# Seven products of quarters in the output half of the last feed-forward layer

## The chip, the cores and the metric

The kernel runs on one core of a Trainium2 chip. The core has a matrix engine (TensorE, PE in the profile, with its weight loads as PEld), three engines for elementwise work (VectorE, DVE; ScalarE, ACT; GpSimd, POOL), SyncE (SP), whose queue issues the transfers, and sixteen transfer engines. Each engine takes its instructions in order and waits for the others through semaphores. On-chip data lie in SBUF; matmuls add into PSUM, eight banks of 512 fp32 columns on 128 partitions. The metric is the time of one execution on the device, in microseconds (us).

## The reference

Two layers over 512 latent tokens of width 1024. The change is in the feed-forward part of the second layer, on latent tokens alone:

```python
def swiglu(h, w_in, w_out):
    gate, up = jnp.split(h @ w_in, 2, axis=-1)
    return (jax.nn.silu(gate) * up) @ w_out
...
f_l = swiglu(modulate(rmsnorm(x, norm_g[i, 2]), sh_fl, sc_fl), ffn_w_in[i], ffn_w_out[i])
x = x + g_fl * rmsnorm(f_l, norm_g[i, 3])
```

The hidden width is 2816. The output half is `act @ w_out`, a product of 512 x 2816 by 2816 x 1024, all in fp32. It is the last matmul of the kernel: after it come one norm, a gain, the addition to x, and the store.

## The kernel before

Every fp32 matrix is split into a high part, which the matmul takes whole, and a low part, the rest. `high` (line 216) is a cast on ScalarE, `low` (line 219) a subtraction on VectorE; a product takes three matmuls: high by high, high by low, low by high (`mm_a`, line 268). Weights come in units of 256 rows by 1024 columns (1 MB) from the list `w`; unit 77 is the first of the eleven of this layer's `w_out` (`F2`, line 36). `Stream` (`ws`, from line 276) fetches units into two buffers `raw` and splits them in halves of 128 rows, each into one of four buffers `w_hi` and `w_lo`. `staged` (line 1092) splits the activations of one 128-row chunk for all 512 tokens into one of four stage buffers `stg` (high part 512 columns, low part 512). Other shared buffers: two `big` ones, six of 1024 columns called `vec`.

`down` (line 1166) is the output half. A unit is two chunks of 128 rows; for each of four blocks of 128 tokens (t) and both halves of 512 output columns, unit and block take 2 x 3 x 2 = 12 matmuls of 128 stationary by 512 moving columns. The eight results y (t, half) fill all eight PSUM banks. Units 0 to 8 run one after the other over the four blocks; the last two units run block by block, so that each block's norm and store (`Chain`, steps `square_y`, `rstd_y`, `gain_y`, `add_x`, `store`) can follow while the next block is multiplied.

`FFN.rest` (line 1501) is the input half. It computes chunk n of the hidden activations (n = 2 to 21), each by seven products of quarters of the input matrix (`product`, line 1433); `gates` (line 1468) writes the chunk, and `act` (line 1290) gives its place: pairs of chunks in one buffer of 2 x 512 columns. T = 10.08 is the planned time of a chunk. The last product of chunk 21 runs after the first output block (`lead`, line 1538), so that the output half begins at the planned time b = T x 20 there.

The order of the work is written by hand: `at(time, step, ...)` (line 582) notes a step with a planned time, or with a rank in a list of names, and `run_plan` (line 592) emits all noted steps in that order. Inside `tc.manual_schedule()` each engine's instructions keep the order in which they are emitted. From the input half of the last layer to the first output block, and again for the last two units, this holds; between these, the units of `down` are ordered by the compiler's own scheduler. The planned times only order the steps: an instruction runs as soon as its engine is free and what it needs is there.

Of the kernel before, what the change touches and what calls it, by code (L numbers as in the profile page):

```python
# [203 lines left out]
def backbone_kernel(ctx: ExitStack, tc: tile.TileContext, a, out):  # L204
# [11 lines left out]
    def high(hi, src):  # L216
        nc.scalar.copy(out=hi, in_=src)  # L217
# [1063 lines left out]
    class FFN:  # L1281
        def __init__(self, layer):
            self.layer, self.u0, self.head_ps, self.slot, self.bank = layer, F1[layer], {}, slot, slot

        def open(self, H):
            self.cm = pool(f"ffn{self.layer}")
            self.p = self.cm.__enter__()
            self.H, self.pairs = H, {}

        def act(self, n):  # L1290

            if n // 2 not in self.pairs:
                self.pairs[n // 2] = self.p.tile([P, 2 * SEQ], F32, name="act", tag="act", bufs=NFF // 2)
            return self.pairs[n // 2][:, (n % 2) * SEQ:(n % 2 + 1) * SEQ]

        def lend(self, u):

            for i in range(2):
                ws.lend(u + i, [self.p.tile([P, D], F32R, name="w_lent", tag="act", bufs=NFF // 2) for _ in range(4)])

        def head(self, t, n):

# [163 lines left out]
            nc.scalar.activation(out=self.g[n][:, i * 256:(i + 1) * 256], in_=self.ps[n, 0 if i else 2], func=AF.Silu)  # L1466

        def gates(self, n):
            nc.vector.tensor_tensor(out=self.act(n), in0=self.c.pop(n)[:, 512:], in1=self.g.pop(n), op=ALU.mult)

        def prepare(self, ch):

# [28 lines left out]
        def rest(self, nxt_of, head, **kw):  # L1501

            T, last, u0, f2 = 10.08, NFF - 1, self.u0, F2[self.layer]
            at(.1, self.head_turn, *self.prev)
            for n in range(2, NFF):
                b = T * (n - 2)
                order = (1, 5, 4, 6, 2, 3, 7) if n > 2 else (1, 2, 5, 6, 3, 7)
                for i, p in enumerate(order):
                    at(b + T / 7 * i, self.product, n - 1 if p == 4 else n, p)
                at(b + 1.7, self.keep, n, 0)  # L1510
                at(b + (3.15 if n > 2 else 4.5), self.keep, n, 1)
                at(b + 6, self.keep, n, 2)
# [12 lines left out]
                at(b + 9.1, ws.fetch, u0 + n + 2 if n < last - 1 else f2 + n - last + 1)  # L1525
            m5 = Ada(self.layer, 5)
            at(T + 5.3, m5.start, nc.gpsimd)
            for k in range(KC):
                at(T * (1 + 2 * k) + 5, m5.fetch_chunk, k)
                at(T * (4 + 2 * k) + .5, m5.add_chunk, k)  # L1530
            at(T * 17, m5.fetch_gain)
            for z in range(2):
                b = T * (18 + z)
                at(b + 2, m5.halve, z * 512, nc.vector)
                at(b + 5.7, m5.total, z * 512, self.bank)
                at(b + 6.6, m5.done, z * 512)

            def lead(take, work):
# [11 lines left out]
            down(f2, NFF // 2, lambda k: staged(self.act(k)), lambda: V[self.layer, 5], nxt_of, head, lead=lead, **kw)  # L1550


    f0 = FFN(0)
# [305 lines left out]
```

## Time and profile before

| | |
|---|---|
| three runs, us | 1137.48, 1137.61, 1141.35 (median 1137.61) |
| profiled execution, us | 1139.76 |
| its span, first to last instruction | 1138.0 |
| granted TensorE clock, mean | 0.999 |
| PE, DVE, ACT, POOL busy, share of the span | 98%, 78%, 50%, 44% |
| first output block of the last layer starts | 1010.7 us |

All rows of the profile come from the one profiled execution. An instruction's duration runs from its start until its result is written; instructions of one engine overlap a little, so back to back they cost less than their durations. Names like `y<-w_hi,st` tell what an instruction writes and reads; L272 is a line of the kernel, and for helpers such as `high` (L217), `low` (L220) and `mm_a` (L272) it is the helper's. "Idle before" is the time in which the engine waited just before an instruction, with the instruction or transfer that ended the wait.

### The profile page before, as it was taken

What the parts mean: (1) busy time and instruction counts of PE and PEld (TensorE: products, weight loads), DVE (VectorE), ACT (ScalarE), POOL (GpSimd) and SP (SyncE); (2) the same over time, 40 slices, a digit from 0 to 9 for tenths busy, and PEclk for the clock granted to TensorE, in tenths of its full rate; (3) what the DMA queues carried; (4) which work ended last, traced back from release to release, by engine and by line L of the source; (5) the groups of instructions that cost most, each with busy time, mean ns of one, the idle gap of its engine ahead of it and who ended that gap; (6) DMA issues with size and microseconds to landing.
All of it is one profiled execution on the core that took longest, in us unless ns stands there. A gap on an engine that the chain in (4) does not pass through costs nothing.

```text
span 1138.0 us, 17909 instructions
## 1 busy us (share of the span) xinstructions
PE 1117.8 (98%) x7134; PEld 984.5 (87%) x7134; DVE 887.5 (78%) x1140; ACT 565.5 (50%) x983; POOL 499.6 (44%) x341
## 2 busy tenths in 40 slices
PE   8999999999999999999999999999999999999997
PEld 5788877768899999998888888888899999998886
DVE  6888988959988989988855767847999998953325
ACT  6357778666544455543324544435545555533322
POOL 2347565514677767630001314006588888700000
PEclk9999999999999999999999999999999999999999
DMA  9642332233134233368753265331243333323221
GB/s 371 261 154 83 123 108 78 75 141 110 65 131 148 97 131 144 130 221 314 297 185 111 77 220 183 119 114 47 70 159 127 113 145 130 131 88 135 74 74 74
DMA packets 29528, 158.19 MB, mean 139 GB/s; under 512 B 3450, under 2 KB 7802, under 8 KB 13700
## 3 DMA queue, kind: packets, MB, share of 16 engines
q1 hardware_dynamic: 29444, 157.04, 38.2%
q8 instruction: 56, 0.92, 0.3%
q14 instruction: 28, 0.23, 0.1%
HBM read 154.94 MB, written 2.10 MB: 138 GB/s over the span
## 4 chain that ended last, share of the span: by engine, by line
PE 88%; DVE 7%; issue 2%; ACT 2%; DMA 1%; SPq 0%; POOL 0%; DVEq 0%; POOLq 0%; ACTq 0%
PE f L1442 33%; PE y L272 27%; PE v L272 3%; PE s_ps L888 3%; PE o_ps L941 2%; PE pT_ps L921 2%; PE u L1684 1%; PE u L1686 1%; PE u L1685 1%; PE q_ps L264 1%; PE q_ps L266 1%; PE q_ps L265 1%; DVE w_lo L220 1%; PE kv L264 1%; DVE a_sum L1368 1%
## 5 line engine op out<-in xcount | busy, mean ns | idle before, releaser
L272 PE MATMUL y<-w_hi,st 128*128 128x512 f32 x928 | 251.4, 389 | 0.0
L220 DVE TENSOR_TENSOR w_lo<-w_raw,w_hi 128x1024 fp32r<-128x1024 f32 (+1 forms) x109 | 154.6, 1419 | 103.6 <-ACT w_hi L217 103.6
L217 ACT CAST w_hi<-w_raw 128x1024 fp32r<-128x1024 f32 x122 | 127.7, 1052 | 177.7 <-PE y L272 124.5
L272 PEld LDWEIGHTS y<-w_hi,st 128*128 128x128 f32 x928 | 173.9, 188 | 36.0
L1399 POOL TENSOR_TENSOR T<-w_raw 128x512 f32<-128x512 f32 x80 | 144.9, 1831 | 96.0 <-DMA w_raw<-in_w 60.5
L1442 PE MATMUL f<-H,w_hi 128*128 128x256 f32 x960 | 178.3, 283 | 2.8 <-DVE fc L1453 2.8
L220 DVE TENSOR_TENSOR w_lo<-T,w_hi 128x1024 fp32r<-128x1024 f32 x80 | 149.0, 1862 | 5.6 <-ACT w_hi L217 5.5
L1442 PEld LDWEIGHTS f<-H,w_hi 128*128 128x128 f32 x960 | 150.1, 192 | 3.7 <-DVE fc L1453 3.2
L245 POOL TENSOR_TENSOR ry<-ry,mhalf 128x1 f32<-128x1 f32 x16 | 9.2, 576 | 327.2 <-DVE ry L242 188.8
L272 PE MATMUL y<-w_lo,st 128*128 128x512 f32 x464 | 144.2, 389 | 0.0
L1442 PE MATMUL f<-H,w_lo 128*128 128x256 f32 x480 | 135.8, 283 | 0.0
L1442 PE MATMUL f<-S,w_hi 128*128 128x256 f32 x640 | 120.0, 285 | 0.3 <-ACT fc L1449 0.3
L217 ACT CAST w_hi<-T 128x1024 fp32r<-128x1024 f32 x80 | 83.6, 1046 | 55.1 <-PE f L1442 29.7
L1449 ACT COPY fc<-f 128x256 f32<-128x256 f32 x120 | 44.8, 373 | 122.9 <-PE f L1442 120.5
L272 PEld LDWEIGHTS y<-w_lo,st 128*128 128x128 f32 x464 | 87.0, 188 | 18.0
L1442 PEld LDWEIGHTS f<-S,w_hi 128*128 128x128 f32 x640 | 99.5, 191 | 0.9 <-ACT fc L1449 0.5
L1442 PEld LDWEIGHTS f<-H,w_lo 128*128 128x128 f32 x480 | 92.1, 192 | 0.0
L1442 PE MATMUL f<-S,w_lo 128*128 128x256 f32 x320 | 90.7, 284 | 0.5 <-DVE w_lo L220 0.5
L366 DVE SCALAR_TENSOR_TENSOR acc<-ada_raw,sc,acc 128x1024 f32<-128x1024 f32 x64 | 84.8, 1325 | 6.4 <-DMA ada_raw<-in_ada 4.2
L1399 POOL TENSOR_TENSOR T<-w_raw,T 128x512 f32<-128x512 f32 x40 | 82.6, 2066 | 3.1
L1399 POOL TENSOR_TENSOR T<-T,w_raw 128x512 f32<-128x512 f32 x40 | 76.3, 1908 | 3.1
L915 POOL TENSOR_SCALAR p<-p,st 128x512 f32<-128x512 f32 (+1 forms) x64 | 55.7, 884 | 42.8 <-DVE st L911 25.1
(238 smaller groups left out, 2437.2 us busy)
## 6 DMA issues: line engine op xcount, KB each, us to landing
w_raw<-in_w SPq DMA_DIRECT2D x83, 1024.0 KB, 4.9
ada_raw<-in_ada SPq DMA_DIRECT2D x32, 1024.0 KB, 4.9
ada<-in_ada SPq DMA_DIRECT2D x8, 1024.0 KB, 12.0
ada_k<-in_ada SPq DMA_DIRECT2D x16, 512.0 KB, 5.7
w_raw<-in_w SPq DMA_DIRECT2D x10, 512.0 KB, 3.7
row<-in_norm_g SPq DMA_DIRECT2D x7, 512.0 KB, 6.5
xin<-in_x SPq DMA_DIRECT2D x4, 512.0 KB
x<-in_x SPq DMA_DIRECT2D x4, 512.0 KB, 7.2
```

What stands on the lines that cost most here:

```text
L217: nc.scalar.copy(out=hi, in_=src)
L220: (eng or nc.vector).tensor_tensor(out=lo, in0=src, in1=hi.bitcast(F32), op=ALU.subtract)
L264: nc.tensor.matmul(dst, lh, rh, start=first, stop=False)
L272: nc.tensor.matmul(dst, l, w[:, n * 512:(n + 1) * 512], start=first and i == 0, stop=last and i == 2)
L366: nc.vector.scalar_tensor_tensor(out=ac, in0=w, scalar=sc[:, k:k + 1], in1=ac, op0=ALU.mult, op1=ALU.add)
L888: nc.tensor.matmul(dst, self.qT[:, j, :], keys, start=i == 0, stop=i == 1)
L915: nc.gpsimd.tensor_scalar(out=p, in0=p, scalar1=self.st[:, 12 + j:13 + j], scalar2=1.0, op0=ALU.mult, op1=ALU.mult)
L921: nc.tensor.transpose(ps[:, j * P:(j + 1) * P], self.probs[j][:, i * P:(i + 1) * P], ident)
L941: nc.tensor.matmul(self.o[z * HD:(z + 1) * HD, c], v, pt[:, c], start=i < 2, stop=i >= self.nb - 2, tile_position=(0, z * HD), skip_group_ ...
L1399: nc.gpsimd.tensor_tensor(out=T[i], in0=x, in1=y, op=op)
L1442: nc.tensor.matmul(dst, l[:, w], r[:, k, :], start=first and k == 0 and j == 0, stop=k == 3 and j == 2, skip_group_check=True)
L1449: nc.scalar.copy(out=self.c[n][:, i * 256:(i + 1) * 256], in_=self.ps[n, 1 if i == 1 else 0])
```

## The change

In the last layer only, units 1 to 8 of the output half (2048 of the 2816 rows) are multiplied by seven products of quarters instead of eight. Units 0, 9 and 10 stay as they were.

- The activations A of units 1 to 8 are kept in four buffers of four quarters of 512 columns: even or odd chunk by the first or second 256 tokens (`fours`, `act`). Buffer p holds two units. The weights B are cut the same way: even or odd chunk by the first or second 512 output columns, and fetched so, 4 units x 512 columns (1 MB) at a time (`fetch7`, eight transfers).
- The seven products, in the order 1, 2, 7, 6, 3, 5, 4, each go over p = 0 to 3; one p is a block of twelve matmuls (`product7`). Per block, `a7_high` and `w7_high` cast a token quarter (512 columns) and a weight quarter (1024 columns) on ScalarE, `a7_low` and `w7_low` subtract on VectorE. They are planned 4.5, 3.9, 3.8 and 2.9 us ahead of the block (U = 2.72).
- Products 7, 6, 3 and 5 take sums of token quarters, made in place by `s7` on VectorE, planned 4.6 us ahead of the block. Products 7 and 5 take sums of two weight quarters, made by `t7` on VectorE; for products 6 and 4, another quarter is added to the sum of product 7 by an accumulating transfer that GpSimd issues (`t7_add`, eight of 512 KB).
- Products 1, 7, 6 and 5 add up in the same two banks. Between them ScalarE saves the state (`save7`), and VectorE adds the saved parts to the banks of the other quarters (`add7`). Unit 0 is multiplied first, in the order of blocks 2, 3, 0, 1, as starting value.
- Units 9 and 10 follow block by block with the norms as before (`plain7`). All of it is noted with `at` and emitted in that order, inside the manual schedule.

```diff
+        def fours(self, g, of=F32):
+            return self.p.tile([P, 2 * D], of, name="act4" if of is F32 else "w_lent", tag="act4", bufs=4)
...
+            if self.fast and 1 <= u < 9:
+                g = (u - 1) // 2
+                if g not in self.four:
+                    self.four[g] = self.fours(g)
+                return self.four[g].rearrange("p (q u s) -> p q u s", q=4, u=2)[:, 2 * (n % 2):2 * (n % 2) + 2, (u - 1) % 2, :]
...
         def gates(self, n):
-            nc.vector.tensor_tensor(out=self.act(n), in0=self.c.pop(n)[:, 512:], in1=self.g.pop(n), op=ALU.mult)
+            x, y, act = self.c.pop(n)[:, 512:], self.g.pop(n), self.act(n)
+            if len(act.shape) == 3:
+                x, y = (v.rearrange("p (q s) -> p q s", q=2) for v in (x, y))
+            nc.vector.tensor_tensor(out=act, in0=x, in1=y, op=ALU.mult)
...
-                at(b + 9.1, ws.fetch, u0 + n + 2 if n < last - 1 else f2 + n - last + 1)
+                if n < last or not self.fast:
+                    at(b + 9.1, ws.fetch, u0 + n + 2 if n < last - 1 else f2 + n - last + 1)
...
+            if self.fast:
+                self.seven(T * (NFF - 2), **kw)
+                return
...
+        def fetch7(self, z, h, of):
+            u = F2[self.layer] + 1 + 4 * h
+            if of is None:
+                if h == 0:
+                    self.tt = hb.tile([P, 8 * D], F32, name="t7", tag="H", bufs=1)
+                t = self.tt[:, (4 + 2 * h) * D:(6 + 2 * h) * D]
+            else:
+                t = of("w7")
+            self.q[z, h] = t
...
+            dma(t.rearrange("p (u c) -> p u c", u=4), a["w"][u:u + 4][:, :, c].rearrange("u p c -> p u c"))
...
+        def w7_high(self, i, p):
+            self.w7[i, p] = hi, lo = tuple(base.tile([P, D], F32R, name=w, tag=w, bufs=4) for w in ("w_hi", "w_lo"))
+            high(hi, self.weights7(i, p))
...
+        def a7_high(self, i, p):
+            self.a7[i, p] = st = stage("s7")
+            high(st[:, 0:512], self.tokens7(i, p))
...
+        def s7(self, name, p):
+            q0, q1, q2, q3 = (self.four[p][:, q * 512:(q + 1) * 512] for q in range(4))
+            if name == "S3":
+                nc.vector.tensor_tensor(out=q1, in0=q0, in1=q1, op=ALU.subtract)
+            elif name == "S4":
+                nc.vector.tensor_tensor(out=q2, in0=q2, in1=q1, op=ALU.add)
+            else:
+                dst, other = (q1, q3) if name == "S2" else (q0, q0)
+                nc.vector.scalar_tensor_tensor(out=dst, in0=q1, scalar=-1.0, in1=other, op0=ALU.mult, op1=ALU.subtract)
...
+        def t7_add(self, p, z):
+            u = F2[self.layer] + 1 + 2 * p
+            nc.gpsimd.dma_start(out=self.tt[:, p * D:(p + 1) * D].rearrange("p (u c) -> p u c", u=2),
+                                in_=a["w"][u:u + 2][:, :, z * D:z * D + 512].rearrange("u p c -> p u c"), accum_op=ALU.add)
+        def bank7(self, i, j):
+            return self.y[j + (2 if i not in (2, 3) else 0)][0 if i in (2, 4) else 1]
+        def product7(self, i, p):
+            (whi, wlo), st = self.w7.pop((i, p)), self.a7.pop((i, p))
+            for j in range(2):
+                for l, (x, w) in enumerate(((0, whi), (0, wlo), (512, whi))):
+                    for z in range(2):
+                        c = x + z * 256 + j * P
+                        nc.tensor.matmul(self.bank7(i, j), st[:, c:c + P], w[:, z * 512:(z + 1) * 512],
...
+        def seven(self, E, **kw):
...
+            for b, z, h, of in ((-9, "11", 0, raw_), (-8.5, "11", 1, big_), (-8, "12", 0, big_), (-1.4, "12", 1, raw_)):
+                at(E + b, self.fetch7, z, h, of)
...
+            at(E, self.plain7, 0, 2)
+            at(E + U, self.product, last, 4)
+            at(E + 4.2, self.plain7, 0, 3)
+            for j in range(2):
+                at(E + 3 + 4 * j, self.save7, "v0", j)
+            at(E + 6.9, self.plain7, 0, 0)
+            at(E + 9.6, self.plain7, 0, 1)
+            b = E + 12.35
+            begin = {}
+            for i in (1, 2, 7, 6, 3, 5, 4):
+                begin[i] = b
+                for p in range(4):
+                    at(b + U * p, self.product7, i, p)
+                    lead = 4.5
+                    for f, d in ((self.a7_high, 0), (self.w7_high, .6), (self.a7_low, .7), (self.w7_low, 1.6)):
+                        at(b + U * p - lead + d, f, i, p)
+                b += 4 * U
+            for p in range(4):
+                at(E + (7.5, 8.7, 15.5, 16.7)[p], self.t7, 1, p)
+                at(E + (18.5, 19.7, 24, 25.2)[p], self.t7, 3, p)
+                for name, i in (("S3", 7), ("S2", 6), ("S4", 3), ("S1", 5)):
+                    at(begin[i] + U * p - 4.6, self.s7, name, p)
+                at(begin[7] + U * p - 1, self.t7_add, p, 0)
+                at(begin[6] + U * p - 1, self.t7_add, p, 1)
+            for h in range(2):
+                at(E + 4.5 + .5 * h, self.fetch7, "21", h, None)
+                at(E + 12.3 + 6 * h, self.fetch7, "22", h, (raw_, big_)[h])
+            for j in range(2):
+                at(begin[2] + .1 + .7 * j, self.save7, "p1", j)
+                at(begin[7] + 2 + 2 * j, self.add7, "c11", j)
+                at(begin[6] - .2 + .1 * j, self.save7, "p7", j)
+                at(begin[6] + 3 + 2 * j, self.add7, "p7", j)
+                at(begin[3] + .1 + .7 * j, self.save7, "u3", j)
+                at(begin[4] + .4 + 1.5 * j, self.add7, "p7d", j)
+                at(begin[4] + 1.2 + 1.5 * j, self.add7, "c12", j)
+                at(begin[4] + 3.6 + .7 * j, self.add7, "c22", j)
+                at(b + .1 + .7 * j, self.add7, "c21", j)
...
+            for v in (9, 10):
+                for h in range(2):
+                    c = b - 8 + 2.4 * (2 * (v - 9) + h)
+                    at(c, ws.high, f2 + v, h)
+                    at(c + 1, ws.low, f2 + v, h, nc.vector)
+                    at(c + .5, self.take7, 2 * v + h)
...
```

More of the change, by code (lines that the diff above doesn't have):

```diff
@@ new lines, in save7, with add7 @@
+        def save7(self, name, j):
+            if j == 0:
+                self.r7[name] = vec("r7")
+            nc.scalar.copy(out=self.r7[name][:, j * 512:(j + 1) * 512], in_=self.bank7(1, j))
+        def add7(self, name, j):
+            r = {k: v[:, j * 512:(j + 1) * 512] for k, v in self.r7.items()}
+            x, c11, c12, c21 = (self.bank7(i, j) for i in (1, 2, 3, 4))
+            out, in0, in1, op = {"c11": lambda: (c11, c11, r["p1"], ALU.add), "p7": lambda: (r["p7"], r["p7"], r["p1"], ALU.subtract),
+                                 "c12": lambda: (c12, c12, r["p7"], ALU.add), "p7d": lambda: (r["p7"], r["p7"], x, ALU.subtract),
+                                 "c22": lambda: (x, r["v0"], x, ALU.subtract), "c21": lambda: (c21, c21, r["u3"], ALU.add)}[name]()
+            nc.vector.tensor_tensor(out=out, in0=in0, in1=in1, op=op)
@@ new lines, in plain7 @@
+        def plain7(self, v, t, ns=(0, 1)):
+            if v == 0:
+                self.y[t] = tuple(self.bank(f"y{t}{n}") for n in range(2))
+            parts = ws.unit(F2[self.layer] + v)
+            for h in range(2):
+                st = self.sts[2 * v + h]
+                for i, (x, w) in enumerate(((0, 0), (0, 1), (512, 0))):
+                    for n in ns:
+                        nc.tensor.matmul(self.y[t][n], st[:, x + t * P:x + (t + 1) * P], parts[h][w][:, n * 512:(n + 1) * 512],
+                                         start=v == 0 and h == 0 and i == 0, stop=v in (0, 10) and h == 1 and i == 2,
+                                         skip_group_check=True)
```

88 lines of the change are left out of this document (83 added, 5 removed).

## The prediction

> **What bounds the kernel now.** I read the chain that ended last first, then the two instruction groups of the output half, then the order and spacing of VectorE's and ScalarE's instructions. The head of the page gives the frame, and the chain in order of time (columns: start us, us, what) the stretch that the change touches.
>
> ```profile
> span 1138.0 us, 17909 instructions
> PE 1117.8 (98%) x7134; PEld 984.5 (87%) x7134; DVE 887.5 (78%) x1140; ACT 565.5 (50%) x983; POOL 499.6 (44%) x341
> ...
> PE 88%; DVE 7%; issue 2%; ACT 2%; DMA 1%; SPq 0%; POOL 0%; DVEq 0%; POOLq 0%; ACTq 0%
> ```
> ```profile
> 1010.70 7.28 PE y L272 x32
> 1017.98 1.43 PE f L1442 x12
> 1019.41 106.80 PE y L272 x471
> ```
> From 1010.7 us on nothing but TensorE is on the chain: one block of output matmuls, the last product of the input half (1.43 us), the other output matmuls. I call the start of that stretch E. The output line's own view, in the window from 900 us, counts them.
>
> ```profile
> L272 PE MATMUL y<-w_hi,st x352: 388/389/397, 1010.5 to 1131.5; 128*128 128x512 f32 x176
> L272 PE MATMUL y<-w_lo,st x176: 389/389/398, 1011.7 to 1131.2; 128*128 128x512 f32 x176
> ```
> 352 + 176 = 528 matmuls; (1131.5 - 1010.5 - 1.43)/527 = 0.227 us each, so a block of twelve takes 2.72 us, and the stretch 528 x 0.227 + 1.43 = 121.2 us. The table by windows shows what the other engines have left there (columns: length, PE, PEld, DVE, ACT, POOL busy, clock, DMA share, GB/s).
>
> ```profile
> 10.00:15.00 5.00, 3.27 (x20) 1.98 (x18) 3.56 (x13) 4.78 (x9) 2.57 (x5) 1.00 1.03 402
> ...
> 1020.00:1040.00 20.00, 20.00 (x90) 16.56 (x89) 9.65 (x11) 7.35 (x11) 0.00 (x0) 1.00 0.42 141
> ...
> 1132.00:1138.00 6.00, 0.00 (x0) 0.00 (x0) 2.23 (x4) 0.65 (x2) 0.55 (x1) 0.85 0.34 130
> ```
> TensorE is full at clock 1.00, VectorE about half busy, GpSimd idle. VectorE's spare half is what the change spends.
>
> **What VectorE and ScalarE charge.** The groups by shape from 1018 us on, then VectorE's and ScalarE's timelines (start us, us, instruction, idle before it and its releaser).
>
> ```profile
> L220 DVE TENSOR_TENSOR w_lo<-w_raw,w_hi 128x1024 fp32r<-128x1024 f32 x19 | 23.2, 1222 | 64.0 <-ACT w_hi L217 64.0
> L217 ACT CAST w_hi<-w_raw 128x1024 fp32r<-128x1024 f32 x19 | 20.0, 1051 | 69.9 <-PE y L272 57.8 <-PE f L1442 8.3 <-issue 3.8
> L220 DVE TENSOR_TENSOR st<-act,st 128x512 fp32r<-128x512 f32 x19 | 13.0, 685 | 0.7 <-ACT st L217 0.7
> L217 ACT CAST st<-act 128x512 fp32r<-128x512 f32 x19 | 11.7, 615 | 1.6 <-DVE act L1469 1.6
> L1122 DVE TENSOR_TENSOR tmp<-y,row 128x512 f32<-128x512 f32 x8 | 5.5, 689 | 6.7 <-ACT junk L235 6.6
> ...
> L1126 DVE SCALAR_TENSOR_TENSOR x<-tmp,ry,x 128x512 f32<-128x512 f32 x2 | 1.4, 749 | 0.1
> ```
> ```profile
> 1007.84 0.69 DVE L220 TENSOR_TENSOR st<-act,st 128x512 fp32r<-128x512 f32 x1 [0.72 <-ACT st L217]
> 1008.45 0.42 DVE L1461 TENSOR_TENSOR f<-f,fc 128x256 f32<-128x256 f32 x1
> 1008.78 1.22 DVE L220 TENSOR_TENSOR w_lo<-w_raw,w_hi 128x1024 fp32r<-128x1024 f32 x1
> 1009.91 0.68 DVE L220 TENSOR_TENSOR st<-act,st 128x512 fp32r<-128x512 f32 x1
> 1010.52 1.22 DVE L220 TENSOR_TENSOR w_lo<-w_raw,w_hi 128x1024 fp32r<-128x1024 f32 x1
> ...
> 1021.55 0.68 DVE L1469 TENSOR_TENSOR act<-fc,silu 128x512 f32<-128x512 f32 x1
> 1022.92 0.69 DVE L220 TENSOR_TENSOR st<-act,st 128x512 fp32r<-128x512 f32 x1 [0.69 <-ACT st L217]
> 1026.95 1.23 DVE L220 TENSOR_TENSOR w_lo<-w_raw,w_hi 128x1024 fp32r<-128x1024 f32 x1 [3.34 <-ACT w_hi L217]
> ```
> ```profile
> 1022.27 0.62 ACT L217 CAST st<-act 128x512 fp32r<-128x512 f32 x1 [1.61 <-DVE act L1469]
> 1025.87 1.05 ACT L217 CAST w_hi<-w_raw 128x1024 fp32r<-128x1024 f32 x1 [2.98 <-PE y L272]
> 1026.83 0.61 ACT L217 CAST st<-act 128x512 fp32r<-128x512 f32 x1
> 1027.34 1.04 ACT L217 CAST w_hi<-w_raw 128x1024 fp32r<-128x1024 f32 x1
> ```
> The reader should take three things. Back to back, a 512-column VectorE instruction costs 0.61 us (1009.91 to 1010.52) and a 1024-column one 1.13 (1008.78 to 1009.91); on ScalarE 0.51 and 0.96. A hand-over costs no more than the producer's duration plus 0.04: VectorE's product at 1021.55 is cast at 1022.27 (0.72 later), that cast's low part starts at 1022.92 (0.65 later), a weight cast of 1025.87 has its low part at 1026.95 (1.08 later). And in a hand-written stretch each engine runs the steps in the order of their planned times: 1007.84 to 1010.52 are stage 0, gate, weight 0, stage 1, weight 1, as planned at E - 3, -2.6, -2.5, -2, -1.5.
>
> **The change, part by part.** *Matmuls.* Units 1 to 8 had 8 x 48 = 384; seven products of four blocks of twelve are 336, of the same shape. 48 x 0.227 = 10.9 us less: the floor is 480 x 0.227 + 1.43 = 110.3 us.
>
> *Splits.* As before, a block needs a token cast and a weight cast on ScalarE (0.51 + 0.96 = 1.47) and two low parts on VectorE (0.61 + 1.13 = 1.74). Alone that hides under a block of 2.72.
>
> *New on VectorE:* eight sums of weight quarters (1.13 each), sixteen sums of token quarters (0.61; eight are three-operand forms, 0.67), twelve adds in PSUM (0.61, from the 689 ns row). That is 9.1 + 10.2 + 7.3 = 26.6 us on top of 28 x 1.74 = 48.7 and of the splits of units 9 and 10 (7.0): 82 us against seven products of 76.2. The floor of VectorE's work by itself almost touches TensorE's.
>
> *The order of these steps* decides. For products 7, 6, 3 and 5 the token sum is planned 4.6 us ahead of its block, the token cast 4.5, the weight cast 3.9, the token low part 3.8, the weight low part 2.9, and the next block's sum follows that. So VectorE runs sum, token low, weight low, next sum; ScalarE runs token cast, weight cast, and the weight cast, which needs no sum, stands behind the token cast, which does. One turn: sum to token cast 0.72, token cast to weight cast 0.51, weight cast to weight low part 1.08, weight low part to the next sum 1.13: 3.45 us, and 3.52 with the three-operand sum. TensorE uses a block up in 2.72. Four buffers of each kind let the splits run three blocks ahead, but they are not ahead when this begins, as the next paragraph shows.
>
> *The sum, from E.* The second block of unit 0 ends at E + 6.9 (2.72 + 1.43 + 2.72); ScalarE's save of its result stands ahead of the first casts, and VectorE's first token low part comes at E + 8.25. Until the first token sum: eight blocks of products 1 and 2 (8 x 1.74 = 13.9), seven weight sums (7 x 1.13 = 7.9), some 0.7 of waits: E + 30.8. Sixteen turns: 8 x 3.45 + 8 x 3.52 = 55.8, and 1.2 for those adds in PSUM that don't fall into a turn's gaps: E + 87.8. Two blocks of product 4 (3.5), then six adds, the token low parts of blocks 3, 4 and unit 9 (nine short ones, 5.5) and three weight low parts (3.4): the last block of product 4 may start at E + 100.3, where the floor had it at 12.35 + 27 x 2.72 = E + 85.8. Then that block and the 96 matmuls of units 9 and 10, 2.72 + 21.8, and 0.2 for the last low part of unit 10: the last matmul ends at E + 125.1 instead of E + 121.2. So 14.8 us of waits against 10.9 saved: +3.9. What follows the last matmul (6 us of one tile's norm and store) is planned the same.
>
> *A save between products 7 and 6.* Both accumulate into the same banks, and ScalarE's copy of product 7 is planned behind the casts of product 6's second block. TensorE waits there for about a turn, some 3.6 us. I cost it at nothing in the end: two blocks stand ready behind it, and the turns set the pace until the end of product 5. If the turns were no bound, it would cost up to 3.6.
>
> *Transfers.* The quarters are 8 MB in place of 8 MB, in rows of 2 KB.
>
> ```profile
> w_raw<-in_w SPq DMA_DIRECT2D x7, 1024.0 KB, 5.0
> w_raw<-in_w SPq DMA_DIRECT2D x4, 512.0 KB, 3.7
> ```
> These are the issues from 690 to 800 us; the second are in rows of 1 KB. Quarter 22 is asked for behind the last use of its buffers and lands, at 5.0 us, about 1.4 and 0.7 us before VectorE comes to it, with SyncE's queue otherwise free. The price is 0 at 5.0 us, and at 2 x 3.7 = 7.4 for a megabyte about 1.7. I take 0.3, since 2 KB lies nearer the first. Dropping one early fetch of unit 1 costs nothing, its quarters come instead.
>
> *Accumulating transfers.* GpSimd issues eight of 512 KB that add a weight quarter to the sum. None is in the trace. Each of the first four may start when its block's low part is done and is wanted 12 us later, with 3.5 us between them; the second four have over 20. The cover is the three turns between. Bounds for one: 3.7 us (the plain 512 KB above), and 12.0 (a megabyte while the queue was full):
>
> ```profile
> ada<-in_ada SPq DMA_DIRECT2D x8, 1024.0 KB, 12.0
> ```
> The first can start one turn into them, at E + 34.4; the fourth's cast stands eight turns and two hand-overs in, at E + 57.4. One at a time, the fourth is late where each takes over (57.4 - 34.4)/4 = 5.8 us; at 12.0 it is 25 us late. A gain is excluded, for nothing waits for them less than for nothing. I take 3.7 and cost 0, as the transfer engines are at a share of 0.42 here and at 1.03 in the row of 10 us. [...]
>
> *Hand-overs* with two waits in one instruction are in no row; I add 0.3. The sum: 3.9 + 0.3 + 0.3 = +4.5 us. The profiled execution took 1139.76 us with its span of 1138.0, 0.2% above the median of 1137.61; the difference is set on the median: 1142.1.
>
> **The rivals.** *The turns don't bind (faster).* If token sums ran a product ahead of their casts, ScalarE would not wait for them. A turn holds 0.61 + 0.61 + 1.13 = 2.35 of work, so 16 x 1.1 = 17 us of waiting goes and the matmuls bound again, but for the save (up to 3.6) and a last low part: -10.9 + 0.2 to -7.1, so about 1128. It decides from a turn of 3.45 - 9.6/16 = 2.85 us down. For it: nothing in the computation ties the sums to that place. Against: rows 1007.84 to 1010.52 keep the written order. 9%.
>
> *The accumulating transfers or the quarters come late (slower).* At 8 us each, one at a time, the fourth lands 9 us late and stops ScalarE, with the save of product 7 behind it: about 1151; at 7.4 us for quarter 22, 1143.8. For it: no such transfer and no GpSimd queue is in the trace. Against: the free transfer engines. 19%.
>
> *The clock falls (slower).* The wait of 3.6 us before product 6 is longer than any of TensorE's in this stretch. In the rows above the clock is 1.00 through 10 to 15 us with TensorE busy for 3.27 of 5, and 0.85 where it has no matmul for 6 us. [...] 4%.
>
> **How the numbers follow.** A measurement here can tell about 0.5% from no change, 5.7 us. The turns that set the pace have the rest, 68%: from +1 (every price at its low end, hand-overs of VectorE overlapping) to +9 (quarter 22 at 7.4 us, 0.1 more per turn for a second wait, 1.6), and some 4 in 10 of that lies above +5.7. Faster: 0.08, nearly all the first rival. Slower: 0.68 x 0.4 + 0.15 + 0.04 = 0.46. Within: 0.46. The range takes that case, the late transfers up to about 9 us, and the edge of the first rival: 1136 to 1152.
>
> **What would show it.** Right: 480 output matmuls; in products 7, 6, 3 and 5 blocks about 3.5 us apart, VectorE idle about 0.75 us ahead of each token low part, released by ScalarE's token cast, and ScalarE idle until VectorE's sum; a TensorE wait of about 3.6 us ahead of product 6, released by ScalarE; products 1 and 2 without a gap over 0.5. Wrong: blocks at 2.72 us through products 7 to 5 (no turn), VectorE idle on a transfer, ScalarE's weight casts of product 6 released by a transfer, or a clock below 1.00 behind the wait.

## Result and profile after

| | before | after |
|---|---|---|
| median, us | 1137.93 (10 runs) | 1143.95 (10 runs, 1142.87 to 1148.27) |
| ratio, 95% interval | | 1.0051 (1.0038 to 1.0064) |
| profiled execution, us | 1139.76 | 1144.66 |
| its span, us | 1138.0 | 1142.9 |
| granted TensorE clock, mean | 0.999 | 0.994 |
| output matmuls | 528 | 480 |
| start of the first to start of the last, us | 121.0 | 126.8 |
| TensorE busy between 1010 and 1110 us | 100.00 | 91.06 |

The kernel is 0.5% slower, 6.0 us by the medians, where 4.5 us were forecast. One matmul in eleven of the output half is gone, and the output half takes 5.8 us longer. (The span grew by 4.9 only, as the first output matmul started 1.3 us earlier, at 1009.2 instead of 1010.5; that difference arises in the first 107 us of the program, which the change doesn't touch.) In all sets of runs together the kernel before took 1137 to 1140 us in 31 of 55 executions and 1140 to 1143 in the others, in shares that differ from set to set, so a ratio below can look up to 0.3% better than one against the 1137.93 above.

The chain of waits of the kernel after, from 1000 us on (start us, us, what):

```profile
1013.53 8.19 PE y L1676 x36
1021.72 10.89 PE y L1649 x48
1033.75 0.96 ACT w_hi L217
...
1062.39 6.44 DMA t<-in_w
1068.91 1.06 ACT w_hi L217
...
1078.23 0.69 DVE act L1619
...
1110.72 1.24 DVE w_lo L220
1112.00 2.60 PE y L1649 x10
1114.60 16.11 PE y L1676 x71
```

Before, TensorE alone was on this stretch. Now the chain leaves it after the 48 matmuls at 1021.72, runs through ScalarE's casts, VectorE's sums and low parts, and once through a transfer (`t<-in_w`, an accumulating one), and comes back for the last block of product 4 at 1112.00. So for some 80 us the preparation by the other two engines sets the pace; TensorE lives on blocks prepared earlier until 1046.55, where its weight loads wait for the first time. The matmul line of `product7` (L1649) says the same (idle time before it, by releaser; a wait of TensorE and that of its weight loads in the same moment are both counted):

```profile
L1649 PE MATMUL y<-w_hi,s x224: 387/389/794, 1021.6 to 1114.2; 128*128 128x512 f32 x112
...
  DVE w_lo L220: 18.2, 24
  ACT r L1657: 7.8, 2
```

A weight's low part ends 11 waits of TensorE (6.5 us) and 13 of its weight loads (11.7 us), and ScalarE's save of a result (`r`, L1657) one of each, 3.7 and 4.1 us: a single stop. One turn in product 3, on VectorE and on ScalarE (start us, us, instruction, idle before it and its releaser):

```profile
1078.23 0.68 DVE L1619 TENSOR_TENSOR act<-act 128x512 f32<-128x512 f32 x1
1079.65 0.69 DVE L220 TENSOR_TENSOR s<-act,s 128x512 fp32r<-128x512 f32 x1 [0.74 <-ACT s L217]
1080.61 1.23 DVE L220 TENSOR_TENSOR w_lo<-w,w_hi 128x1024 fp32r<-128x1024 f32 x1 [0.26 <-ACT w_hi L217]
1081.75 0.69 DVE L1619 TENSOR_TENSOR act<-act 128x512 f32<-128x512 f32 x1
```
```profile
1079.00 0.62 ACT L217 CAST s<-act 128x512 fp32r<-128x512 f32 x1 [0.98 <-DVE act L1619]
1079.53 1.04 ACT L217 CAST w_hi<-w 128x1024 fp32r<-128x1024 f32 x1
1082.52 0.62 ACT L217 CAST s<-act 128x512 fp32r<-128x512 f32 x1 [1.95 <-DVE act L1619]
```

Token sum (L1619), 0.77 later its cast, 0.53 later the weight cast, 1.08 later the weight's low part, 1.14 later the next sum: 3.52 us for a block that TensorE uses up in 2.72. VectorE idles for 0.74 to 0.77 in nearly every turn because ScalarE has not cast what VectorE has just summed, and ScalarE idles for 1 to 2 us because VectorE has not summed yet.

GpSimd's issues of the accumulating transfers, and the DMA rows of the window from 985 us:

```profile
1043.61 1.36 POOL L1637 DMA_DIRECT2D t<-in_w  x1 [51.46 <-DVE act L1617]
1049.88 1.23 POOL L1637 DMA_DIRECT2D t<-in_w  x1 [4.91 <-DVE y L1666]
1056.18 1.21 POOL L1637 DMA_DIRECT2D t<-in_w  x1 [5.08 <-DVE s L220]
1062.39 1.23 POOL L1637 DMA_DIRECT2D t<-in_w  x1 [5.00 <-DVE act L1622]
```
```profile
w<-in_w SPq DMA_DIRECT2D x6, 1024.0 KB, 6.3
t<-in_w POOLq DMA_DIRECT2D x8, 512.0 KB, 6.0
```
```profile
1068.91 1.05 ACT L217 CAST w_hi<-t 128x1024 fp32r<-128x1024 f32 x1 [2.54 <-DMA t<-in_w]
```

One transfer takes 6.0 us from issue to landing, and these issues stand 6.2 to 6.3 us apart: each starts 0.2 to 0.3 us after the one before has landed, although the low parts of product 7 that they wait for start 3.5 to 3.8 us apart (1041.72, 1045.27, 1049.07, 1052.60). The fourth lands at 1068.83 and ScalarE's weight cast has waited 2.54 us for it. The table by windows (length; PE, PEld, DVE, ACT, POOL busy; clock; DMA share; GB/s) shows what happens between products 7 and 6:

```profile
1055.00:1060.00 5.00, 1.48 (x7) 0.87 (x5) 3.52 (x5) 3.03 (x5) 1.21 (x1) 0.86 0.44 67
1060.00:1065.00 5.00, 4.81 (x11) 3.80 (x12) 3.98 (x6) 2.21 (x4) 1.23 (x1) 0.50 0.43 61
1065.00:1070.00 5.00, 5.00 (x23) 4.09 (x21) 1.95 (x5) 1.68 (x2) 0.85 (x1) 0.96 0.53 91
```
```profile
1060.19 1.22 PE L1649 MATMUL y<-w_hi,s 128*128 128x512 f32 x2 [3.71 <-ACT r L1657]
```

TensorE waits 3.71 us for the save, and then runs at a clock of 0.50; the losses of the three rows, 0.14 + 0.50 + 0.04 of five microseconds each, are 6.8 us at half. The fall begins during the wait, at about 1058.6.

### The profile page after: what moved, and what is told of

Read it like the earlier page. It is cut to its first block, busy times and chain, and to the rows that moved or that the text cites. A ratio compares the mean times of both kernels' runs of the same rounds, so it can differ in the third digit from the quotient of the medians.

```text
span 1142.9 us, 17937 instructions
## 1 busy us (share of the span) xinstructions
PE 1114.9 (98%) x7086; PEld 977.1 (85%) x7086; DVE 934.6 (82%) x1200; ACT 590.0 (52%) x1015; POOL 501.1 (44%) x349
## 4 chain that ended last, share of the span: by engine, by line
PE 81%; DVE 9%; ACT 4%; issue 3%; DMA 2%; POOL 0%; SPq 0%; DVEq 0%; POOLq 0%; ACTq 0%
PE f L1456 33%; PE y L272 17%; PE s_ps L888 3%; PE v L272 3%; DVE w_lo L220 3%; PE o_ps L941 2%; PE y L1676 2%; PE pT_ps L921 2%; DMA ada<-in_ada 2%; PE q_ps L264 1%; PE u L1909 1%; PE u L1911 1%; PE u L1910 1%; PE q_ps L266 1%; ACT w_hi L217 1%
## 5 line engine op out<-in xcount | busy, mean ns | idle before, releaser
L1413 POOL TENSOR_TENSOR T<-w_raw 128x512 f32<-128x512 f32 x80 | 141.0, 1782 | 104.7 <-DMA w_raw<-in_w 67.9
L217 ACT CAST w_hi<-w_raw 128x1024 fp32r<-128x1024 f32 x106 | 111.2, 1054 | 114.4 <-PE y L272 66.3
L220 DVE TENSOR_TENSOR w_lo<-w_raw,w_hi 128x1024 fp32r<-128x1024 f32 (+1 forms) x93 | 133.4, 1435 | 40.1 <-ACT w_hi L217 40.1
L272 PE MATMUL y<-w_hi,st 128*128 128x512 f32 x576 | 155.9, 390 | 0.0
L220 DVE TENSOR_TENSOR w_lo<-T,w_hi 128x1024 fp32r<-128x1024 f32 x80 | 146.7, 1834 | 4.8 <-ACT w_hi L217 4.7
L272 PEld LDWEIGHTS y<-w_hi,st 128*128 128x128 f32 x576 | 107.8, 188 | 22.3
L272 PE MATMUL y<-w_lo,st 128*128 128x512 f32 x288 | 88.7, 389 | 0.0
L1413 POOL TENSOR_TENSOR T<-T,w_raw 128x512 f32<-128x512 f32 x40 | 72.1, 1802 | 3.1
L1649 PE MATMUL y<-w_hi,s 128*128 128x512 f32 x224 | 62.5, 400 | 3.7 <-ACT r L1657 3.7
```

Of the source, the lines that this page charges most:

```text
L220: (eng or nc.vector).tensor_tensor(out=lo, in0=src, in1=hi.bitcast(F32), op=ALU.subtract)
L272: nc.tensor.matmul(dst, l, w[:, n * 512:(n + 1) * 512], start=first and i == 0, stop=last and i == 2)
L1413: nc.gpsimd.tensor_tensor(out=T[i], in0=x, in1=y, op=op)
L1649: nc.tensor.matmul(self.bank7(i, j), st[:, c:c + P], w[:, z * 512:(z + 1) * 512], start=i == 1 and p == 0 and l == 0 and z == 0, stop=p == ...
```

## Experiments

Four explanations compete for the 16.7 us of waiting (10.9 saved + 5.8 lost): the turns, the late transfers, the save between products 7 and 6, and the clock that falls behind it. Two kernels, `e2_sums_early_no_add` and `e3_no_add`, leave the accumulating transfers out, so that their products 6 and 4 multiply by the weight sums of product 7. Medians of single kernels compare with 1143.95 us of the changed one (1144.34 when it was measured again); ratios are to the kernel before, run on the same chip.

### Token sums earlier

```diff
-                    at(begin[i] + U * p - 4.6, self.s7, name, p)
+                    at(begin[i] + U * p - 8, self.s7, name, p)
```

> The token sums are planned 8 us ahead of their block instead of 4.6, so that each stands before the casts of the block ahead of it. Theory of the turns: a token cast no longer waits for a sum that waits for the block before it; VectorE's waits of 0.75 us ahead of the token low parts go, and the blocks of products 7, 3 and 5 follow each other at 2.72 us. Then the accumulating transfers, one every 6.3 us in the changed kernel's trace, bind at product 6: TensorE waits there some 5 to 8 us, released through a weight cast by a transfer. Against the changed kernel about -8.4 us, against the kernel before about -2.4 (near 1135.5). Rival, VectorE is simply full with 82 us of work in 76: its waits move but the blocks stay near 3.2 us and the time changes by less than 3 us (near 1142). Rival, the transfers alone made the loss: no change against the changed kernel.

Measured: 1136.38 us, ratio 0.9971 (0.9957 to 0.9986), output stretch 119.4 us instead of 126.8. The mere place of sixteen sums in the written order is worth 7.6 us, so the turns are a large part of the loss. VectorE's row of sums and low parts has closed up, until a transfer stops it (VectorE, then ScalarE, of this run):

```profile
1051.07 1.22 DVE L220 TENSOR_TENSOR w_lo<-t,w_hi 128x1024 fp32r<-128x1024 f32 x1
1052.20 0.68 DVE L1622 SCALAR_TENSOR_TENSOR act<-act 128x512 f32<-128x512 f32 x1
1052.80 0.68 DVE L220 TENSOR_TENSOR s<-act,s 128x512 fp32r<-128x512 f32 x1
1055.83 1.23 DVE L220 TENSOR_TENSOR w_lo<-t,w_hi 128x1024 fp32r<-128x1024 f32 x1 [2.35 <-ACT w_hi L217]
```
```profile
1054.76 1.04 ACT L217 CAST w_hi<-t 128x1024 fp32r<-128x1024 f32 x1 [3.48 <-DMA t<-in_w]
...
1060.95 1.05 ACT L217 CAST w_hi<-t 128x1024 fp32r<-128x1024 f32 x1 [3.66 <-DMA t<-in_w]
...
1067.27 1.04 ACT L217 CAST w_hi<-t 128x1024 fp32r<-128x1024 f32 x1 [4.75 <-DMA t<-in_w]
```

Low part, sum, token low part now stand 1.13 and 0.60 us apart, with nothing between. But the preparation reaches each accumulated weight before its transfer has landed, so the second limit, one transfer in 6.2 us, now shows on three casts in a row.

### The same without the accumulating transfers

```diff
-                    at(begin[i] + U * p - 4.6, self.s7, name, p)
+                    at(begin[i] + U * p - 8, self.s7, name, p)
-                at(begin[7] + U * p - 1, self.t7_add, p, 0)
-                at(begin[6] + U * p - 1, self.t7_add, p, 1)
```

> As with the early sums, and the eight accumulating transfers are left out, so products 6 and 4 are multiplied by the wrong sums of weights. Theory of the turns: with neither turns nor transfers nothing holds TensorE but the floor of the matmuls and about 1 us of VectorE's waits; TensorE without a wait over 1 us from product 7 to product 4; against the kernel before about -10 us (near 1128). If VectorE's 82 us of work were the bound by themselves, -3 to -6 (1132 to 1135).

Measured: 1127.70 us, ratio 0.9890 (0.9874 to 0.9906), output stretch 110.1 us, which is the floor that the prediction worked out (110.3). TensorE has no wait left in the products: between 1010 and 1110 us it is busy for 100.00 us at clock 1.00.

So the turns and the transfers together are the whole loss. The wait for the save is no third one: it goes when the preparation runs ahead.

### Only the transfers left out

```diff
-                at(begin[7] + U * p - 1, self.t7_add, p, 0)
-                at(begin[6] + U * p - 1, self.t7_add, p, 1)
```

> The changed kernel with only the eight accumulating transfers left out (products 6 and 4 then use wrong sums of weights). Theory of the turns with the fourth transfer late: the one wait of ScalarE for a transfer (2.5 us) goes and nothing else; -1.8 to -2.5 us against the changed kernel, so +3.5 to +4.2 against the kernel before (near 1142). Rival, the transfers are the main loss: back to the kernel before or below it (1128 to 1138).

Measured: 1141.75 us, ratio 1.0015 (1.0001 to 1.0028), stretch 124.3: with the turns in place the late transfers cost 2.2 us. With the sums early they cost 8.7 (1136.38 against 1127.70). And the turns, which cost 7.6 with the late transfers behind them, cost 14.1 without them (1141.75 against 1127.70): they are the main cost.

### The save between products 7 and 6 earlier

```diff
-                at(begin[6] - .2 + .1 * j, self.save7, "p7", j)
+                at(begin[6] - 2.5 + .1 * j, self.save7, "p7", j)
```

> The changed kernel with the copies of product 7's banks planned 2.5 us ahead of product 6 instead of 0.2, so that they stand before the casts of product 6's second block. Theory of the turns: TensorE's wait of 3.7 us before product 6 shrinks to about 1 and the clock behind it (0.81 in that stretch) stays nearer 1.00, but the same time is waited for in the blocks that follow, since the splits set the pace; total within 1 us of the changed kernel (+5 to +6.5 against the kernel before, near 1143.5). Rival, the wait and the slower clock behind it cost what they show: 3 to 5 us less than the changed kernel (near 1139.5).

Measured: 1144.07 us, ratio 1.0042 (1.0025 to 1.0060), stretch 126.3. The two waits of TensorE there:

```profile
1056.60 0.73 PE L1649 MATMUL y<-w_hi,s 128*128 128x512 f32 x2 [0.20 <-ACT r L1657]
...
1069.46 0.73 PE L1649 MATMUL y<-w_hi,s 128*128 128x512 f32 x2 [2.33 <-ACT w_hi L217]
```

The wait of 3.71 us is down to 0.20, and the time is the same: product 6 began earlier and ran into its preparation instead. The largest single wait on TensorE in the whole stretch cost nothing. On the clock this run decides nothing: it is 1.00 between 1055 and 1065 us, but goes to half for 3.4 us from 1070.7 on, behind the wait of 2.33.

### Room for two transfers

Why does GpSimd issue one at a time? The kernel sets `dynamic_dma_scratch_size=1024`. Theory A: the space that this sets aside has room for one such transfer (that it holds the transfers' descriptors is the author's reading of the name; no trace shows what is in it). Theory B: such transfers follow one another whatever the setting. The edit sets 1152.

```diff
-    nc = _bacc.Bacc(..., dynamic_dma_scratch_size=1024)
+    nc = _bacc.Bacc(..., dynamic_dma_scratch_size=1152)
```

> [...] In the changed kernel's trace GpSimd issues an accumulating transfer only about 0.2 us after the one before has landed (one every 6.3 us), though what it needs from VectorE is done earlier. Theory A, the space holds the descriptors of one transfer but not of two: with an eighth more two fit, GpSimd issues the second within some 1.5 us of the moment its block is split, and ScalarE's wait for the fourth transfer (2.5 us) goes; time about -2 us against the changed kernel. Theory B, the transfers wait for one another for another reason, or the space is rounded: still one every 6.3 us and no change.

Measured in one execution: 1141.95 us, stretch 124.3.

```profile
1043.45 1.35 POOL L1637 DMA_DIRECT2D t<-in_w  x1 [51.45 <-DVE act L1617]
1046.63 1.20 POOL L1637 DMA_DIRECT2D t<-in_w  x1 [1.83 <-DVE w_lo L220]
1050.47 1.22 POOL L1637 DMA_DIRECT2D t<-in_w  x1 [2.64 <-DVE w_lo L220]
```
```profile
1055.00:1060.00 5.00, 1.27 (x6) 0.73 (x4) 3.70 (x5) 3.03 (x5) 1.45 (x2) 0.84 0.89 141
1060.00:1065.00 5.00, 4.99 (x12) 3.93 (x13) 4.01 (x6) 2.01 (x3) 1.55 (x2) 0.50 0.94 158
```

GpSimd now waits for VectorE's low part, as the code says, and issues 3.2 to 3.8 us apart (the fourth at 1054.02). Landing still takes 6.0 us, two are under way together, and the DMA share doubles from 0.44 to 0.89. So it is the setting that decides, as in theory A: with 1024 the issues stood 6.2 to 6.3 us apart. No cast waits for a transfer any more, and the time is that of the run without the transfers (1141.75).

### Each add as two halves

```diff
+            for i in range(2):
-            nc.gpsimd.dma_start(out=..., in_=a["w"][u:u + 2]..., accum_op=ALU.add)
+                nc.gpsimd.dma_start(out=..., in_=a["w"][u + i]..., accum_op=ALU.add)
```

> The changed kernel with each accumulating transfer of 512 KB issued as two of 256 KB. Theory A (space for descriptors): two or three halves are in flight, GpSimd issues the second half right behind the first (about 1.2 us), and the pairs come every 3.5 us with the blocks; the wait for the fourth goes. [...]

Measured in one execution: 1142.13 us, stretch 124.3. Of the halves three are under way at once (an estimate from the issues and the median): two are issued from 1043.57 on and the third at 1046.75, 3.2 us behind the first, and landing takes 5.4 us (median). So with 1024, too, more than one of them can be under way, and no cast waits for a transfer. By accident it is the cleanest look at the clock, too (L1650 is line L1649 of the others):

```profile
1060.00:1065.00 5.00, 4.86 (x21) 4.06 (x22) 4.00 (x6) 2.15 (x4) 1.87 (x3) 1.00 0.83 135
```
```profile
1060.14 0.73 PE L1650 MATMUL y<-w_hi,s 128*128 128x512 f32 x2 [3.69 <-ACT r L1658]
```

The same wait, 3.69 us, but the clock stays at 1.00 through the five microseconds in which it was at 0.50 in the run above, behind 3.74. The two stretches are equal (124.3 us each): a clock at half for 6.8 us (0.16 + 0.50 of the two rows above, and the rest behind them) costs nothing here that shows; the blocks behind it wait for their preparation with either clock.

### Sums earlier and room for two

The edits of `e1_sums_early` and `e5_ring` together.

> Early token sums and the larger space for descriptors. Under theory A nothing is left that holds TensorE: as without the accumulating transfers, near 1128, 10 us below the kernel before. Under theory B the same as the early sums alone: 1136, with three waits of TensorE at product 6.

Measured: 1127.42 us, ratio 0.9886 (0.9854 to 0.9918), stretch 110.1. The whole computation, 1.1% faster than before by the ratio, 0.9% against the 1137.93 us of the result. The 100 us from 1010 on, and the stretch in which VectorE has most to do:

```profile
1010.00:1110.00 100.00, 100.00 (x449) 83.06 (x448) 87.58 (x110) 57.76 (x82) 10.42 (x9) 1.00 0.48 121
```
```profile
1040.00:1055.00 15.00, 15.00 (x68) 12.43 (x67) 15.00 (x20) 9.89 (x14) 4.99 (x4) 1.00 0.74 117
```

TensorE never waits. VectorE has no gap either between 1040 and 1055 us: in that stretch the two engines are balanced.

### Another order of the products instead of more room

Product 3 takes no accumulated weights, so putting it between 7 and 6 gives the transfers eleven microseconds more. The sums are early here, too, and `dynamic_dma_scratch_size` is the 1024 of the changed kernel.

```diff
-            for i in (1, 2, 7, 6, 3, 5, 4):
+            for i in (1, 2, 7, 3, 6, 5, 4):
-                    at(begin[i] + U * p - 4.6, self.s7, name, p)
+                    at(begin[i] + U * p - (19.9 if name == "S2" else 8), self.s7, name, p)
-                at(begin[6] - .2 + .1 * j, self.save7, "p7", j)
+                at(begin[3] + .1 + .7 * j, self.save7, "p7", j)
-                at(begin[3] + .1 + .7 * j, self.save7, "u3", j)
+                at(begin[5] - 2.5 + .1 * j, self.save7, "u3", j)
```

> Early token sums, and product 3 moved between 7 and 6, so that the first four accumulating transfers have a product (10.9 us) more, and the copies of product 7's banks are made while product 3 runs. At one transfer every 6.3 us the fourth lands 25 us behind the first issue, and is wanted some 26 us behind it: no wait or under 1 us. Theory of the turns and late transfers: TensorE without a wait over 1 us, near 1128 to 1129, 9 to 10 us below the kernel before. If the transfers slowed VectorE or the casts by their traffic rather than by being late, it would stay near 1133 to 1136.

Measured: 1128.83 us, ratio 0.9894 (0.9868 to 0.9920), stretch 111.3. GpSimd still issues the first four 6.1 to 6.3 us apart and ScalarE still waits 4.9 us in all for transfers, but TensorE waits only once, for 0.23 us, and its weight loads four times, 1.6 us in all; the stretch is 1.2 us over the shortest. The late transfers need either room or distance.

### Which link of the turn costs what

These two have room for two transfers and leave the sums 4.6 us ahead of their blocks; only the order of the four splits behind the sum changes. First the weight cast ahead of the token cast, so that ScalarE makes it while VectorE sums:

```diff
-                    for f, d in ((self.a7_high, 0), (self.w7_high, .6), (self.a7_low, .7), (self.w7_low, 1.6)):
+                    for f, d in ((self.w7_high, -.05), (self.a7_high, 0), (self.a7_low, .7), (self.w7_low, 1.6)):
```

> The token sums stay 4.6 us ahead; only the order of the two casts is changed, weight cast ahead of token cast on ScalarE, with the larger space for descriptors. Theory of the turns: the weight cast no longer stands in the turn, so a turn is sum to token cast 0.72, token cast to token low part 0.65, the two low parts 0.61 + 1.13: 3.1 to 3.2 us in place of 3.54 measured; blocks of products 3 and 5 that far apart, VectorE still idle 0.75 us ahead of each token low part but no longer ahead of the weight low part. With the larger space alone the kernel took 1141.95; 16 turns x 0.35 = 5.5 less, and a little lost where product 2 starts: 1136 to 1138. Rival, it is the place of the sums alone that counts: no change (1142). Rival, any break of the order frees it all: 1127 to 1128.

Measured: 1137.42 us, ratio 0.9972 (0.9954 to 0.9990).

```profile
1070.28 0.69 DVE L1619 TENSOR_TENSOR act<-act 128x512 f32<-128x512 f32 x1
1071.71 0.69 DVE L220 TENSOR_TENSOR s<-act,s 128x512 fp32r<-128x512 f32 x1 [0.74 <-ACT s L217]
1072.33 1.22 DVE L220 TENSOR_TENSOR w_lo<-w,w_hi 128x1024 fp32r<-128x1024 f32 x1
1073.46 0.69 DVE L1619 TENSOR_TENSOR act<-act 128x512 f32<-128x512 f32 x1
```

The wait of 0.26 us ahead of the weight's low part is gone and that of 0.74 stays: 3.18 us a turn (1070.28 to 1073.46), against 3.52. It is worth 4.5 us against the one execution of `e5_ring`. Then the weight's low part ahead of the token's, too, so that VectorE does it while ScalarE casts the tokens:

```diff
-                    for f, d in ((self.a7_high, 0), (self.w7_high, .6), (self.a7_low, .7), (self.w7_low, 1.6)):
+                    for f, d in ((self.w7_high, -.05), (self.a7_high, 0), (self.w7_low, .7), (self.a7_low, 1.6)):
```

> As the run with the weight cast first, and on VectorE the weight low part ahead of the token low part too; the sums still 4.6 us ahead of their block. Theory of the turns: the weight low part fills the time in which ScalarE casts the token sum, a turn is sum, weight low, token low back to back, 0.61 + 1.13 + 0.61 = 2.36 us, under a block's 2.72; no wait of TensorE over 0.5 us from product 7 to product 4; 1127 to 1128.5, the same as with the early sums and the larger space. Rival, the sums stand too near their blocks whatever the order: 1134 or above.

Measured: 1128.60 us, ratio 0.9886 (0.9863 to 0.9910).

```profile
1073.24 0.68 DVE L1622 SCALAR_TENSOR_TENSOR act<-act 128x512 f32<-128x512 f32 x1
1073.84 1.22 DVE L220 TENSOR_TENSOR w_lo<-t,w_hi 128x1024 fp32r<-128x1024 f32 x1
1074.98 0.68 DVE L220 TENSOR_TENSOR s<-act,s 128x512 fp32r<-128x512 f32 x1
1075.58 0.68 DVE L1622 SCALAR_TENSOR_TENSOR act<-act 128x512 f32<-128x512 f32 x1
```

No idle time is left on VectorE in these rows: 2.34 us a turn, less than TensorE's 2.72. The sums stand as close ahead of their blocks as in the changed kernel; work that doesn't hang on the hand-over now fills it.

### The changed kernel once more

> The changed kernel as it is, on the chip of these runs: 5 to 7 us above the kernel before in its undisturbed runs, near 1143.9, so that the others of this call can be set against it.

Measured: 1144.34 us, ratio 1.0043 (1.0027 to 1.0060), beside the two runs above on one chip.

## Why the prediction came out as it did

The time, 1143.95 us, lies in the range of 1136 to 1152 and 1.9 us above the forecast; at a ratio of 1.0051 it is at the very edge between "within 0.5%" and "slower", which the prediction gave 0.46 each.

- **Matmuls and floor: right.** 480 matmuls; the floor of 110.3 us was reached at 110.1 in `e2_sums_early_no_add` and `e7_sums_early_ring`.
- **The turns: right, in mechanism and nearly in size.** The forecast had 3.45 us for a turn and 3.52 with the three-operand sum; thirteen of the sixteen take 3.52 to 3.56, and the other three hold an add in PSUM or the late transfer. The hand-over from sum to cast costs 0.77 instead of 0.72. The three-operand sum is no dearer than the other (0.68 us, not 0.749, the row the working leaned on). The first token sum came 30.1 us after the start of the output half (30.8 forecast), and the idle 0.75 us ahead of each token low part, released by ScalarE's token cast, is there. The low part of product 5's last weight ended 60.15 us after the first sum, where 55.8 + 1.2 = 57.0 was forecast; 2.3 of the 3.15 us are the late transfer, the rest the longer turns. From there until the last block of product 4 had its weight's low part it took 12.5 us (12.4 forecast). `e1_sums_early` and `e11_weight_first` show the turns from two sides: take the dependence out of the row or fill the gap, and they go.
- **Accumulating transfers: the mis-sized term.** Costed at nothing with 3.7 us each, they took 6.0, one in 6.3. The prediction's own bound said that one at a time the fourth is late from 5.8 us each: at 6.3 that is four times 0.5 = 2.0 us late, and VectorE's wait was 2.30, ScalarE's 2.54. Its doubt was right in form too: "no such transfer and no GpSimd queue is in the trace". The argument against, that the transfer engines are free, failed: they had room (share 0.44), but GpSimd issued none until the one before had landed, 6.2 to 6.3 us apart; with 1152 in place of 1024 it issued them 3.2 to 3.8 us apart and the share was 0.89 (`e5_ring`). The term is worth about 2 us (2.2 in `e3_no_add`, 2.0 in `e5_ring`). That the total came within 1.5 us of the forecast is in part luck, as other terms make up for some of it: the last block of product 4 could go on 102.8 us after the output half began, 100.3 forecast, and that is + 3.15 for the sixteen turns and - 0.7 for the first sum; what follows took about 0.5 less, as two matmuls of that block had run already; and 0.6 had been set aside for hand-overs and 2 KB rows. The rival of the late transfers, with 8 us each, was right in kind and four times too large.
- **The save: right.** The wait forecast at 3.6 us was 3.71, and costing it at nothing because the turns set the pace was right: without it the time is the same (`e4_save_early`).
- **The clock: it fell, at no cost that shows.** The rival had the right wait: at its end the clock was at 0.50, for 6.8 us in all, and at 1066 us it was back at 1.00. The turns behind absorbed it: in `e6_halves`, where it did not fall, the stretch is as long as in `e5_ring` (124.3 us each), where it was at half for 6.8 us, too.
- **Quarters in 2 KB rows:** a megabyte landed in 6.3 us over the whole window, between the two bounds of 5.0 and 7.4, and no instruction on the chain waited for one.
- **The faster rival: priced right, its condition not met.** "If token sums ran a product ahead of their casts", about 1128. `e7_sums_early_ring` puts them ahead and takes 1127.42, but the sums alone gave 1136.38: the rival had left the transfers out, most of whose cost the turns had hidden. "A turn of 2.85 us" as the point from which it decides is bracketed only: 3.18 us gives 1137.42, 2.34 gives 1128.60.
- **The signs.** Those for being right were there: 480 matmuls, the spacing, the idle time with its releasers, the wait ahead of product 6, and no gap in products 1 and 2. But two of those for being wrong were there as well: a weight cast of product 6 released by a transfer (the fourth, 2.54 us), and a clock below 1.00 behind the wait. The first is the mis-sized term; the second cost nothing that shows.
- **VectorE's work:** 82 us against 76.2 is more than TensorE's, not "almost" as much. It fits all the same (`e7_sums_early_ring`), since the 82 hold the splits of units 9 and 10, whose 21.8 us of matmuls the 76.2 leave out.

## What to carry to other kernels

When two engines that keep to the written order hand work back and forth, price the turn, not the busy time: VectorE was 78% busy between 1010 and 1110 us here and still set the pace, and moving independent work (the weight's cast and low part) into the hand-over, or planning the sums 3.4 us earlier, was worth 13 to 15 us once two transfers had room (1141.95 to 1128.60 and 1127.42), and without one instruction less. Before a limit is taken away, look for the one that stands just behind it: the transfers cost 2 us behind the turns and 9 without them. The longest wait in a profile may be free: ask whether what follows it is waiting for something else anyway.

## What the runs showed of the hardware

- **The setting `dynamic_dma_scratch_size` decided whether GpSimd's transfers overlapped.** With 1024 a second accumulating transfer of 512 KB (2 KB rows) wasn't issued until the first had landed, the first four 6.2 to 6.3 us apart (the changed kernel); with 1152 (`e5_ring`), or as halves of 256 KB with 1024 (`e6_halves`), they overlapped, and the first four (or the first four pairs) followed the work, 3.2 to 3.9 us apart. Why 1024 lets one through and 1152 two is not shown: no run has another value. In the trace of the changed kernel such a wait looks like GpSimd idle "until" some unrelated VectorE instruction (4.91 to 5.08 us of it ahead of the second to fourth issue); it is known by the issue that comes 0.2 to 0.3 us after the landing.
- **An accumulating transfer of 512 KB landed in 6.0 us** (the median of eight), a plain one of before, issued by SyncE and also of 512 KB, in 3.7; an accumulating one of 256 KB, with others under way, in 5.4. Each took GpSimd 1.2 us to issue (0.88 for 256 KB).
- **The clock fell for 3.4 us or for 6.8, and the length of the wait alone didn't decide which.** At half rate the runs spent 6.8 us (the changed kernel and `e5_ring`, with waits of 3.71 and 3.74), about 3.4 us (`e3_no_add`, with 3.73; `e10_weight_cast_first`, with 2.40; `e4_save_early`, with 2.33; twice in `e1_sums_early`, with 2.82, and with 1.97 and one of 0.53 after it), or none (`e6_halves`, with 3.69). The rows of the first such wait in `e1_sums_early` and of its second:

```profile
1055.00:1060.00 5.00, 3.66 (x10) 2.86 (x11) 2.43 (x3) 2.29 (x4) 1.15 (x1) 0.68 0.66 98
1060.00:1065.00 5.00, 5.00 (x23) 4.15 (x22) 2.96 (x5) 1.57 (x2) 1.23 (x1) 0.97 0.44 51
...
1070.00:1075.00 5.00, 5.00 (x17) 3.93 (x16) 5.00 (x8) 3.47 (x6) 1.22 (x1) 0.66 0.55 100
```

The losses of clock are 0.32 + 0.03 and 0.34 of five microseconds, so 3.5 and 3.4 us at half. A wait of 1.97 us and one of 0.53 behind it were enough for a fall, then, and one of 3.69 was not. The clock of single microseconds adds this: in the 3.4 us (as long as the shorter falls) ahead of the start of each of these seven falls TensorE had waited for 1.8 to 3.2 us in all (an estimate from the start of the fall and the waits ahead of it). Why none followed in `e6_halves` stays open.
